# One more expert with 64 token slots, and another order of the experts, in a two-layer decoder trunk

## The chip, the cores and the metric

The kernel runs on one core of one Trainium2 chip. The metric is the device time of one execution in microseconds (us), the median of several runs. A measurement of this kernel can tell a change of about 0.2% (3 us) from none.

## What is computed

Two decoder layers over 256 tokens of width 1024, in float32. The change touches only the channel mixer of the second layer, a mixture of eight SwiGLU experts of which each token uses two:

```python
def _moe(h, w_router, w1, w3, w2):
    logits = (h @ w_router).astype(jnp.float32)
    top_v, top_i = lax.top_k(logits, TOP_K)          # TOP_K = 2 of N_EXPERTS = 8
    wts = jax.nn.softmax(top_v, axis=-1)
    ...
    for e in range(N_EXPERTS):
        y = y + gates[..., e:e + 1] * _swiglu(h, w1[e], w3[e], w2[e])
```

`_swiglu(h, w1, w3, w2)` is `(silu(h @ w1) * (h @ w3)) @ w2`, with a hidden width of 3584. One expert's three matrices are 3 x 1024 x 3584 floats, 42 MiB. 256 tokens times 2 make 512 choices. With the given inputs, the reference's routing gives expert 0 65 tokens and the other seven, sorted, 89, 75, 65, 63, 60, 48 and 47.

## The kernel before, in words

**Ahead of the experts** come dilated attention, the dense mixer and sliding-window attention; the change leaves them alone. The router then counts the tokens of each expert on the chip. Expert 0 always has rank 0. The other seven get ranks 1 to 7 by falling count (`route`, L1343).

**Slots.** An expert of rank r is computed for a fixed number of token slots, `CAPS[r]`, 96 or 64 (L31). `Expert` (L1140) builds a 0/1 matrix P on VectorE that says which token sits in which slot. For 64 slots it also copies P's 64 columns into the second half of the tile (L1152). `gather` (L1155) multiplies the normalised tokens by P on TensorE, which packs the expert's tokens into `xb`. `combine` (L1176) brings the results back to their tokens with P's transpose and adds them to the stream x. If a count is above its slots, `most` (L1441) is above 0, and a conditional block (L1466) computes all eight experts again for the tokens left over.

**Products of one expert.** The hidden width is cut into chunks of 1024, 1024, 1024 and 512 (`moe_chunks`). `hidden` (L1217) makes the products with w1 and w3 of one chunk into PSUM tiles H, `hidden_tail` (L1242) applies SiLU and the product and transposes the result on TensorE, and `output` (L1265) makes the products with w2 into PSUM tiles Y. Each TensorE instruction holds 32 token slots as the stationary operand and streams up to 512 weight columns, so the number of instructions goes with slots/32:

```python
for i in range(2):
    for g in range(ng):                    # ng = slots // 32
        mm32(H[i], g, x[g], a[i], **go)
    for g in range(4 - ng):
        mm32(H[i], ng + g, x[g], b[i], **go)
if ng == 3:                                # 96 slots: a third PSUM tile
    ...
```

That is 12 instructions for each 128 rows of a chunk of w1 and w3 with 96 slots and 8 with 64, and in `output` 6 and 4 for each 128 rows of w2. The trace shows each float32 product as two passes. The order on TensorE is H of chunk 0, H of chunk 1, Y of chunk 0, H of chunk 2, Y of chunk 1, H of chunk 3, Y of chunk 2, H of the next expert's chunk 0, Y of chunk 3.

**Weights.** All weights come through SyncE's DMA queue in tiles of 1 MiB, in the order in which TensorE uses them (`Stream`, L152). An expert takes 42 tiles, whatever its slots. The tiles rotate through 17 buffers: 5 called raw, 2 mwa, 10 mwb. SyncE issues a tile's DMA when the tile that held the buffer before has been used, and waits there in order. The eight experts run in two halves of four (`by_turn`, L1438 and L1511), in the order of `TURNS` (L32). Between the halves all engines read `most` and branch around the conditional block; by then the first 17 tiles of the second half have been asked for. In the last expert the ten mwb buffers are given up (`moe_cut`) after its third chunk's w1 and w3, and its last tiles and the four of the final gate matrix (`ple_w_gate`) pass through the other seven.

Of the kernel before, what the change touches and what calls it, by code (L numbers as in the profile page):

```python
# [27 lines left out]
FE = 3584  # L28
NE = 8

CAPS = (96, 96, 96, 96, 96, 96, 64, 64)  # L31
TURNS = (0, 6, 1, 2, 3, 4, 5, 7)  # L32
CAP = 96
BIG = 512.0
NRAW = 5
# [300 lines left out]
def trunk(ctx, tc, x, p, attn_norm, ffn_norm, a_w_qkv, a_w_o, kv_norm, kv_w, b_w_q, b_sinks,  # L336
# [70 lines left out]
    def add_moe(s, seq, at=None, extra=None):  # L407


        prev = None  # L410
        where = 0
        for j, item in enumerate(list(seq) + [None]):
            if item is not None:
                e, f0, fn = item
                nr = s.width * 128 // fn
                for r in range(0, D, nr):
                    for w in (moe_w1, moe_w3):
                        s.add(expert_rows(w, e, r, nr, f0, fn), "raw")
            if j == at:
                s.add(extra, "raw")  # L420
                where = len(s.specs)
            if prev is not None:
                e, f0, fn = prev
                for r in range(0, fn, s.width * 128 // D):
                    s.add(expert_rows(moe_w2, e, f0 + r, s.width * 128 // D, 0, D), "raw")
            prev = item
        return where
# [4 lines left out]
    def moe_seq(es):  # L432
        return [(e, f0, fn) for e in es for f0, fn in moe_chunks]
# [17 lines left out]
    moe0 = len(st.specs)  # L451
    ranks = [(r,) if r else 0 for r in TURNS]
    add_moe(st, moe_seq(ranks[:4]))
# [463 lines left out]
    if True:  # L917
# [127 lines left out]
        count, total, capx, capt = (rt.tile([128, NE], F32, name=n) for n in ("count", "total", "capx", "capt"))  # L1045
        for r, c in enumerate(CAPS):
            vec.memset(capt[:, r:r + 1], float(c))
# [3 lines left out]
        def warm(n):  # L1051

            t = scr()
            v = n_f1.h0[0]
            for _ in range(n):
                mm(t, v[:, :128], v, start=True, stop=True)
# [286 lines left out]
    def route():  # L1343
# [14 lines left out]
        if WARM2:  # L1358
            warm(WARM2)
        first.append(Expert(CAPS[0], posm[:, :, 0:1], by_rank[1][:, :, 0:1]))  # L1360
        vec.tensor_copy(count, ps[:, 16:24])
# [43 lines left out]
    def expert_pools(sb, ps, k):  # L1405

        nonlocal moep, psH, psY, psB
        moep = pool(f"moe{k}", 2, sb, side="right")
        psH = pool(f"psH{k}", 1, ps, space=PSUM)
        psY = pool(f"psY{k}", 1, ps, space=PSUM)  # L1410
        psB = pool(f"psS{k}", 2, ps, space=PSUM)
# [4 lines left out]
    def by_turn(turns, then={}, **kw):  # L1416

        def make(r):
            return lambda: Expert(CAPS[r], *(v[:, :, r:r + 1] for v in by_rank)) if r else first[0]

        experts([make(r) for r in turns], then=then, **kw)

    def find():

        flow.until(lambda: ranked)
        for r in TURNS:
            if r:
# [9 lines left out]
    expert_pools(moes, banks, 1)  # L1437
    by_turn(TURNS[:4], {(0, 0): find})  # L1438

# [70 lines left out]

    by_turn(TURNS[4:], {(3, PLE_AT - 1): load_p1, (3, PLE_AT): proj_p1}, nxt=n_p1.half)  # L1511
    st.phase(7)
# [89 lines left out]
```

## Time and profile before

| | |
|---|---|
| median of 3 runs | 1594.5 us (1593.62 to 1595.17) |
| the profiled execution | 1597.32 us |
| its span, first to last instruction | 1595.6 us |
| TensorE (PE) busy in it | 1542.3 us, 97% |
| DMA, mean of the span | 286 GB/s |
| expert weight tiles | 336 of 1024 KB |
| experts, first half | from about 631 us |
| experts, second half | from about 1095 us |
| tail after the last expert's hidden stages (final gate, norm, output) | from about 1530 us |

A row of a view by stretches gives, for each engine, its busy time in a stretch and in brackets its instructions; then the share of its clock that TensorE was granted, the busy share of the 16 DMA engines, and what they moved. A row of the chain gives a start, a duration and what ran: the chain is the work that ended last, followed back from the end, so it shows what the end waited for at each moment.

### The profile page before, as it was taken

What the parts mean: (1) busy time and instruction counts of PE and PEld (TensorE: products, weight loads), DVE (VectorE), ACT (ScalarE), POOL (GpSimd) and SP (SyncE); (2) the same over time, 40 slices, a digit from 0 to 9 for tenths busy, and PEclk for the clock granted to TensorE, in tenths of its full rate; (3) what the DMA queues carried; (4) which work ended last, traced back from release to release, by engine and by line L of the source; (5) the groups of instructions that cost most, each with busy time, mean ns of one, the idle gap of its engine ahead of it and who ended that gap; (6) DMA issues with size and microseconds to landing.
All of it is one profiled execution on the core that took longest, in us unless ns stands there. A gap on an engine that the chain in (4) does not pass through costs nothing. (4 is left out here: it accounts for less than half of the span.)

```text
span 1595.6 us, 29196 instructions
## 1 busy us (share of the span) xinstructions
PE 1542.3 (97%) x12326; PEld 874.3 (55%) x12326; DVE 549.3 (34%) x1286; ACT 437.4 (27%) x857; POOL 11.3 (1%) x22
## 2 busy tenths in 40 slices
PE   7999999999999999999999999987999999999977
PEld 6999889788888876333342333333343343343326
DVE  6776677654446793100201102111000200201124
ACT  5555555554445672100100101000000000001123
POOL 0000000000000000000000000000000000000000
PEclk9999999999999999999999999997999999999997
DMA  9544445565554434999999999996999999999880
GB/s 275 150 138 138 120 139 186 154 227 180 190 190 146 142 109 189 409 403 408 409 402 409 404 407 409 403 408 262 387 360 383 368 343 386 367 345 401 324 330 27
DMA packets 214586, 455.71 MB, mean 286 GB/s; under 512 B 15440, under 2 KB 97232, under 8 KB 214448
## 3 DMA queue, kind: packets, MB, share of 16 engines
q1 hardware_dynamic: 214128, 453.31, 77.0%
q8 instruction: 98, 1.61, 0.4%
q0 software_dynamic: 176, 0.40, 0.1%
q14 instruction: 40, 0.33, 0.1%
q10 hardware_dynamic: 144, 0.07, 0.0%
HBM read 452.69 MB, written 1.05 MB: 284 GB/s over the span
## 5 line engine op out<-in xcount | busy, mean ns | idle before, releaser
L1137 PE MATMUL H<-mwb,xb 128*32 128x512 f32 (+1 forms) x3320 | 337.7, 538 | 0.4 <-DMA mwb<-in_moe_w 0.4
L135 DVE TENSOR_TENSOR wlo<-raw,whi 128x768 fp32r<-128x768 f32 (+1 forms) x180 | 188.6, 1080 | 117.7 <-ACT whi L135 117.5
L135 DVE TENSOR_TENSOR sa<-sa,H 128x512 f32<-128x512 f32 (+1 forms) x32 | 19.9, 621 | 591.2 <-PE H L1137 591.2
L1137 PEld LDWEIGHTS H<-mwb,xb 128*32 128x32 f32 x3320 | 110.8, 110 | 203.0 <-issue 180.0
L135 ACT ACTIVATE whi<-raw 128x768 fp32r<-128x768 f32 (+1 forms) x180 | 162.0, 945 | 110.9 <-PE scr L347 61.3
L135 ACT ACTIVATE sa<-H 128x512 f32<-128x512 f32 (+1 forms) x32 | 17.4, 544 | 637.3 <-PE H L1137 637.3
L1137 PE MATMUL H<-raw,xb 128*32 128x512 f32 (+1 forms) x1560 | 168.5, 545 | 1.0 <-DMA raw<-in_moe_w 1.0
L1137 PE MATMUL Y<-mwb,hT 128*32 128x512 f32 x1304 | 150.8, 594 | 0.0
L1137 PE MATMUL Y<-raw,hT 128*32 128x512 f32 x904 | 105.6, 593 | 0.0
L1137 PEld LDWEIGHTS H<-raw,xb 128*32 128x32 f32 x1560 | 52.6, 110 | 95.5 <-issue 83.3
L347 PE MATMUL acc<-whi,xT0h 128*128 128x384 f32 (+2 forms) x296 | 104.1, 352 | 0.0
L347 PE MATMUL acc<-wlo,xT0h 128*128 128x384 f32 (+2 forms) x296 | 101.7, 344 | 1.6 <-DVE wlo L135 1.6
L347 PE MATMUL acc<-whi,xT0l 128*128 128x384 f32 (+2 forms) x296 | 101.5, 343 | 0.0
L347 PE MATMUL acc<-whi,xT1h 128*128 128x384 f32 (+2 forms) x280 | 98.2, 351 | 0.3 <-ACT xT1h L135 0.3
L347 PE MATMUL acc<-whi,xT1l 128*128 128x384 f32 (+2 forms) x280 | 93.8, 335 | 0.2 <-DVE xT1l L135 0.2
L347 PE MATMUL acc<-wlo,xT1h 128*128 128x384 f32 (+2 forms) x280 | 93.4, 334 | 0.0
L1137 PEld LDWEIGHTS Y<-mwb,hT 128*32 128x32 f32 x1304 | 41.7, 110 | 88.7 <-issue 86.7
L1137 PE MATMUL H<-mwa,xb 128*32 128x512 f32 (+1 forms) x752 | 88.9, 534 | 0.0
L1137 PEld LDWEIGHTS Y<-raw,hT 128*32 128x32 f32 x904 | 29.2, 110 | 62.4 <-issue 60.4
L347 PEld LDWEIGHTS acc<-whi,xT0h 128*128 128x128 f32 x296 | 56.5, 191 | 4.9 <-issue 2.3
L347 PEld LDWEIGHTS acc<-wlo,xT0h 128*128 128x128 f32 x296 | 56.3, 190 | 4.5 <-DVE wlo L135 2.3
L347 PEld LDWEIGHTS acc<-whi,xT0l 128*128 128x128 f32 x296 | 56.2, 190 | 3.0 <-DVE xT0l L135 0.3
(222 smaller groups left out, 1878.9 us busy)
## 6 DMA issues: line engine op xcount, KB each, us to landing
mwb<-in_moe_w SPq DMA_DIRECT2D x190, 1024.0 KB, 16.0
raw<-in_moe_w SPq DMA_DIRECT2D x104, 1024.0 KB, 13.9
mwa<-in_moe_w SPq DMA_DIRECT2D x42, 1024.0 KB, 15.1
raw<-in_a_w_qkv SPq DMA_DIRECT2D x144, 256.0 KB, 3.9
raw<-in_dense_w SPq DMA_DIRECT2D x33, 1024.0 KB, 5.0
raw<-in_ple_w_gate SPq DMA_DIRECT2D x8, 1024.0 KB, 9.6
raw<-in_a_w_o SPq DMA_DIRECT2D x4, 1024.0 KB, 5.1
raw<-in_b_w_q SPq DMA_DIRECT2D x4, 1024.0 KB, 5.2
```

What stands on the lines that cost most here:

```text
L135: f(*a, **k)
L347: nc.tensor.matmul(dst, lhsT, rhs, **kw)
L1137: nc.tensor.matmul(dst, xs, w, start=start, stop=stop)
```

## The change

The sixth entry of `CAPS`, the slots of rank 5, goes from 96 to 64, and `TURNS` is rearranged:

```diff
-CAPS = (96, 96, 96, 96, 96, 96, 64, 64)
-TURNS = (0, 6, 1, 2, 3, 4, 5, 7)
+CAPS = (96, 96, 96, 96, 96, 64, 64, 64)
+TURNS = (0, 5, 1, 2, 6, 3, 4, 7)
```

By slots, the order of the eight was 96, 64, 96, 96 and 96, 96, 96, 64. It is now 96, 64, 96, 96 and 64, 96, 96, 64. In the first half the instructions are the same ones (another expert's weights are read in the second place, and the table of slots holds another number). In the second half the first expert has 64 slots where it had 96. SyncE's list of DMAs is the same, row for row.

TensorE at the start of the second half, where the first expert's hidden stage begins (H_23211 to H_23213 are its PSUM tiles, mwb and raw the weight tiles, xb the gathered tokens):

```order
 L1137 MATMUL H_23211<-mwb,xb 32x512 x4
 L1137 MATMUL H_23212<-raw,xb 32x512 x4
-L1137 MATMUL H_23213<-mwb,xb 32x512 x2
-L1137 MATMUL H_23213<-raw,xb 32x512 x2
-L352 MATMUL scr<-ident,P 96x128 x2
+L352 MATMUL scr<-ident,P 128x128 x2
 L1137 MATMUL H_23211<-mwb,xb 32x512 x4
 L1137 MATMUL H_23212<-raw,xb 32x512 x4
-L1137 MATMUL H_23213<-mwb,xb 32x512 x2
-L1137 MATMUL H_23213<-raw,xb 32x512 x2
```

The third PSUM tile and its 4 of 12 instructions are gone for every 128 rows of this expert's weights.

VectorE at the same place, just after the branch: it builds P, on which TensorE's gather waits there. Before:

```order
L135 TENSOR_SCALAR P<-iota,posr 128x96 x2
L135 CAST PT<-scr 96x256
L135 TENSOR_TENSOR sa<-sa,H_23212 128x512
L135 TENSOR_TENSOR sb<-sb,H_23213 64x512
L135 COPY hT<-scr 128x256
```

Now:

```order
L135 TENSOR_SCALAR P<-iota,posr 128x64
L135 COPY P<-P 128x64
L135 TENSOR_SCALAR P<-iota,posr 128x64
L135 COPY P<-P 128x64
L135 CAST PT<-scr 128x256
L135 TENSOR_TENSOR sa<-sa,H_23212 128x512
```

Two copies stand between and after the two parts of P, and the work on the third PSUM tile (sb, and its hT) is gone.

## Rows read from the trace of the kernel before

**Rows 1.** The page: busy time of the engines; the chain that ended last, by line.
```profile
PE 1542.3 (97%) x12326; PEld 874.3 (55%) x12326; DVE 549.3 (34%) x1286; ACT 437.4 (27%) x857; POOL 11.3 (1%) x22
...
PE H L1137 17%; PE Y L1137 8%; PE scr L347 2%; PE acc L347 1%; DMA raw<-in_ple_w_gate 1%; PE scr L1258 1%; DVE wlo L135 0%; PE scr L352 0%; ACT xb L135 0%; DVE gate L135 0%; DVE h L135 0%; DVE x L135 0%; ACT gate L135 0%; DVE yl L135 0%; POOLq L1599 0%
```

**Rows 2.** Stretches: the first half, the halt at the branch, the second half.
```profile
core 0: us, PE busy (x) PEld busy (x) DVE busy (x) ACT busy (x) POOL busy (x), PEclk, DMA share, GB/s
640.00:1080.00 440.00, 432.04 (x4205) 152.31 (x4197) 53.91 (x101) 36.56 (x66) 0.00 (x0) 1.00 1.03 406
1093.00:1100.00 7.00, 7.00 (x61) 3.43 (x64) 0.42 (x1) 0.65 (x2) 0.00 (x0) 0.94 0.01 3
...
1120.00:1480.00 360.00, 359.22 (x3516) 127.84 (x3512) 44.50 (x79) 29.03 (x54) 0.00 (x0) 1.00 0.97 372
```

**Rows 3.** What SyncE's DMA queue waited for, 1100 to 1500 us: total, times, longest.
```profile
SPq L230 <- PE H L1137: 198.9, 63, 7.5
SPq L230 <- PE Y L1137: 107.2, 43, 7.1
```

**Rows 4.** Stretches of PE: 64 slots, 96 after it, two of the second half's 96.
```profile
743.50:828.60 85.10, 84.96 (x820) 1.00 1.03 406
828.60:948.90 120.30, 118.58 (x1161) 1.00 1.03 407
1207.30:1328.20 120.90, 120.57 (x1178) 1.00 0.97 365
1328.20:1448.90 120.70, 120.58 (x1180) 1.00 0.96 366
```

**Rows 5.** What PE itself waited for by DMA, 828 to 949 us.
```profile
PE H L1137 <- DMA raw<-in_moe_w: 1.0, 1, 1.0
PE H L1137 <- DMA mwb<-in_moe_w: 0.4, 1, 0.4
```

**Rows 6.** The chain in the second half: start us, us, what.
```profile
1231.47 0.98 PE scr L1258 x8
...
1270.36 20.60 PE H L1137 x192
1290.96 1.97 PE scr L347 x16
...
1411.90 1.93 PE scr L347 x16
...
1417.21 10.44 PE Y L1137 x96
1427.65 10.36 PE H L1137 x192
...
1466.22 0.59 PE scr L1258 x4
...
1494.78 13.73 PE H L1137 x128
...
1516.02 7.00 PE Y L1137 x64
1523.02 6.52 PE H L1137 x120
```

**Rows 7.** Timeline of VectorE and TensorE at the branch; P's readers there (min/median/max ns).
```profile
1088.52 0.45 DVE L135 TENSOR_SCALAR P<-iota,posr 128x96 f32<-128x96 f32 x2 [5.77 <-DVEq L1466]
...
1088.94 6.14 PE L347 MATMUL scr<-P,xn 128*128 128x96 f32 x32 [6.97 <-DVE P L135]
...
L347 PEld LDWEIGHTS scr<-P,xn x32: 192/333/333, 1088.9 to 1094.7; 128*128 128x128 f32 x32
```

**Rows 8.** Timeline of SyncE's DMA issues: at the branch, and in the last expert.
```profile
1054.36 46.90 SPq L230 DMA_DIRECT2D mwb<-in_moe_w  x10
1101.51 10.65 SPq L230 DMA_DIRECT2D raw<-in_moe_w  x5
...
1488.40 7.23 SPq L230 DMA_DIRECT2D mwa<-in_moe_w  x2
1515.61 7.84 SPq L230 DMA_DIRECT2D raw<-in_moe_w  x5
```

**Rows 9.** Line L230's DMAs from 600 us on: time from issue to landing.
```profile
DMA to landing us min/median/max: 5.0/15.2/21.8
```

## The prediction

> **What bounds the kernel now.** The page says TensorE is busy 97% of the span and heads the chain that ended last, with the experts' H and Y products as its largest parts [rows 1]. That is an average, so the next view is by stretches [rows 2]. It shows two different states. In the first half of the experts the DMA engines run without a break, at 406 GB/s. In the second half they move 372 GB/s and have pauses, although TensorE is as busy as before. What SyncE waits for tells which of the two limits the second half: for 199 us on H products and 107 us on Y products [rows 3]. It waits until TensorE has used a tile and its buffer comes free. So in the second half TensorE sets the pace, and the transfers follow. There TensorE waited for a transfer for only 1.4 us in all, in the expert after the 64-slot one [rows 5], so both are close to their limits. The second half is where the change takes work away.
>
> **What the change removes.** One expert of 96 slots becomes one of 64. The stretches give its worth in one step. From one expert's first hidden product to the next one's takes 120.9 and 120.7 us for 96 slots in the second half, and 85.1 us for the 64 slots of the first half, whose neighbours were both 96 as well [rows 4]: 35.7 us less. The last Y products of an expert fall into the next one's stretch, so that stretch is shorter too: 120.3 us, of which TensorE was busy 118.58 [rows 4]. In it TensorE waited for transfers for 1.4 us [rows 5]. Without that it is 118.9, or 1.9 less than 120.8. Sum: 37.6 us.
>
> The same from below, as a check [rows 6]. H of a full chunk is 192 passes in 20.60 us with 96 slots and 128 in 13.73 with 64, so 6.87 less, three times: 20.6. The half chunk is 192 passes of 256 columns in 10.36 us; two thirds of it is 6.9, so 3.5 less (of those 128 passes the chain shows 120 in 6.52 us). Y is 96 passes in 10.44 us against 64 in 7.00, so 3.44 for a full chunk, and 3.5 chunks: 12.0. The transposes of a hidden chunk take 0.98 us against 0.59; 0.39 times 3.5 is 1.4. Together 37.5 us. All of it lies on TensorE, and in the second half TensorE's time is the chain without a gap, so the end moves by the same amount as long as the weights keep up (below).
>
> **What it adds and moves.** VectorE builds P at the branch with two copies more. One stands between the two parts of P. TensorE's gather starts right after the first part and would need the second part at its second product [rows 7]. The trace has no such copy; the bounds are 0 and 0.27 us, the length of one part of P (0.45 us for two that overlap). I take 0.2 us, since a copy of 64 columns is nearest to a part of P with 96.
>
> The gather at the branch has 64 columns in place of 96. It took 6.14 us for 32 passes, 0.192 us each, and the shortest weight load there took the same 192 ns, so the loads, which don't change, set its pace [rows 7]. Bounds: 0, and a third of 6.14 us, 2.0 us less. A pair of warm gathers decides: 16 passes took 1.97 us with 96 columns and 1.93 us with 64 [rows 6]. I take 0.1. The Trainium skill (TensorE: Matmul & The Clock Gate, "Wait — 56ns, not 53.3ns?") says that back-to-back matmuls start a number of columns divided by the clock apart; by that the gather would shrink by a third, and the sum be 2 us better. The warm pair shows 2% and not a third, so it is not followed here.
>
> The work of ScalarE and VectorE on the third PSUM tile goes too. I cost that at nothing: TensorE is busy 359.2 of 360 us beside it [rows 2]. In the first half a 64-slot expert stands between two of 96, and TensorE has 0.14 us of idle time in its 85.1 [rows 4]; a new wait at these seams is bounded by that, and the other seams keep their neighbours.
>
> **Whether the weights keep up.** This is the term that can eat the gain. The transfers do not shrink: 42 tiles for each expert. At 406 GB/s [rows 2] a tile of 1.0486 MB takes 2.58 us, 108.5 us for an expert. A 96-slot expert takes longer than that (120.8), a 64-slot one less (85.1). So a 64-slot expert eats into the tiles that wait in the buffers, 23 us of them, and a 96-slot one gives back 12.
>
> At the branch all 17 buffers have been filled: DMA falls to 3 GB/s at 1093 to 1100 us [rows 2]. Transfers start again when TensorE releases the first pair of tiles, at 1100.9 (the last of ten issues that end at 1101.3) [rows 8]. A transfer alone takes 5.0 us [rows 9], so tile 18 lands at 1105.9 and each one after it 2.58 us later if SyncE never waits for long. TensorE reaches the second expert of the half, which needs tile 42, at 1207.3 before [rows 4] and at about 1171.6 after. Tile 42 lands at 1105.9 + 24 x 2.58 = 1167.8. That is 3.8 us early. In the two 96-slot experts that follow the lead grows again by about 12 us each. The other close place is in the last expert, up to tile 161, the last one before SyncE halts for the seven buffers that are left (it waited there from about 1495 to 1515.6 before [rows 8]). Tile 161 lands at 1105.9 + 143 x 2.58 = 1474.8, and is needed when the last hidden chunk begins: 1523.0 before [rows 6], 1485.5 after. That is 10.7 us early. From there on each transfer is started by a release, as before, and the tail keeps its shape. So the end should move by the full amount, but the pace may not fall below 143 tiles in 379.6 us, 2.655 us each or 395 GB/s.
>
> **The sum.** -37.6 + 0.2 - 0.1 = -37.5 us. Of the profiled execution's 1597.3 us that leaves 1559.8. The same difference from the median of the runs, 1594.5, gives **1557.0 us**.
>
> **The rivals.**
>
> *The transfers become the bound.* Below 395 GB/s the end is late by 143 x (1048.6 / pace - 2.655) us with the pace in GB/s. For it: the second half moved only 372 GB/s. At that pace the tile takes 2.819 us, the end is 23.4 us late, and the time is 1580. Against it: SyncE was waiting for buffers in those 372 [rows 3], and without such long waits it held 406 GB/s over 440 us [rows 2]. The Trainium skill (HBM Reference, "Specifications") speaks against the change: it gives a core about 358 GB/s of its memory's bandwidth. By that the tile would take an estimated 2.93 us, the end would be 39 us late and the gain gone, at 1596. It is a share for two cores at work at once, and the trace's 406 GB/s with one at work stands against it. A mild form, 400 to 393 GB/s, costs 0 to 2 us. I give the whole case 0.07, most of it for the mild form to 1562.
>
> *The overflow block runs.* This is the one that ends slower. It decides at L1466: if the expert of rank 5 has 65 tokens or more, all eight experts are computed again. 336 tiles at 2.58 us are 867 us more at least, about 2424 us. The counts speak against it: 60 tokens of rank 5 with these inputs, four below the point. The chance is 0.01.
>
> *The narrow expert is no shorter, or the seams between widths wait.* For it would speak idle time around the 64-slot expert of the first half; there is 0.14 us [rows 4]. If each of the two new neighbours waited as long as the gather waits at the branch for P (0.4 us) or some us for a combine, 1558 to 1562. If the expert were not shorter at all, the time would stay at 1594.5. The first has 0.04, the second 0.01.
>
> **How the numbers follow.** The forecast gets 0.87. Its own bounds are 2 us less (the gather, all of its third), 1 us either way for the two sums and the runs' own spread (1593.6 to 1595.2), and upward 0.2 us of copies and the 1.4 us of short waits that the first half had. That makes 1554.5 to 1559.5. The range reaches on to the mild forms of the first and third rival, 1562. About 0.2% of this kernel, 3 us, is what a measurement can tell from no change. Faster by more than that: the forecast, the third rival's seams and all of the first rival but its far end, 0.97. Within: the far end of the first rival and the expert that is not shorter, 0.015. Slower: the overflow and what I have not thought of, 0.015.
>
> **What would show it.** In the changed kernel's profile the first half should look the same. In the second half the stretch of the first expert should be about 76 us where it was 112 (1095.0 to 1207.3), the next one about 119, the other two as before. The DMA rate from 1105 us on should be at 400 GB/s or more, against 372, with far less waiting of SyncE on H and Y products. TensorE's waits for transfers should stay at some 2 us in all. The SyncE halt in the last expert should be there still, shorter than 20 us, since the transfers arrive with less lead. The tail after the last hidden chunk should have the same length. Wrong would be: waits of TensorE for mwb, raw or mwa tiles of 5 us or more, at the second expert's start or in the last expert, with a DMA rate under 395 GB/s; a second pass over the weights after the branch; or idle TensorE at the seams between widths, ended by VectorE or ScalarE.

## The result, and the profile after

The changed kernel takes **1558.87 us** (median of four runs, 1557.69 to 1559.65). Beside it the kernel before took 1594.84 us (four runs, 1593.62 to 1595.63). The ratio is 0.9773, with a 95% interval of 0.9761 to 0.9785, so the change saves 36.0 us. The forecast was 1557.0 us with a range of 1554.5 to 1562.

The profiled execution of the changed kernel took 1557.69 us, and its span is 1555.9 us. Its stretches of TensorE, cut at the experts' first hidden products, at the last hidden chunk and at the end (columns as in [rows 2]):

```profile
1093.90:1171.90 78.00, 77.86 (x755) 27.73 (x758) 3.69 (x8) 5.72 (x11) 0.00 (x0) 0.98 0.95 372
1171.90:1290.30 118.40, 118.06 (x1160) 42.16 (x1156) 11.69 (x21) 8.67 (x16) 0.00 (x0) 1.00 1.03 407
1290.30:1411.00 120.70, 120.59 (x1182) 42.94 (x1178) 16.09 (x29) 9.72 (x18) 0.00 (x0) 1.00 1.03 406
1411.00:1484.90 73.90, 73.90 (x608) 23.48 (x604) 10.41 (x15) 8.91 (x15) 0.00 (x0) 1.00 0.95 370
1484.90:1555.90 71.00, 50.14 (x374) 31.30 (x366) 27.88 (x48) 24.02 (x49) 2.83 (x4) 0.87 0.45 171
```

Three of the same stretches before, the ones that are not among [rows 4]:

```profile
1095.00:1207.30 112.30, 111.96 (x1121) 40.42 (x1124) 7.74 (x16) 7.98 (x15) 0.00 (x0) 1.00 0.92 349
1448.90:1522.80 73.90, 73.90 (x608) 23.50 (x604) 10.38 (x15) 8.91 (x15) 0.00 (x0) 1.00 0.91 354
1522.80:1595.60 72.80, 51.63 (x374) 32.14 (x366) 28.06 (x48) 24.01 (x49) 2.83 (x4) 0.84 0.43 166
```

Read down, they say where the time came from:

| Stretch | before, us | after, us | difference | forecast |
|---|---|---|---|---|
| up to the second half's first hidden product | 1095.0 | 1093.9 | -1.1 | +0.1 |
| second half, first expert (now 64 slots) | 112.3 | 78.0 | -34.3 | -35.7 |
| second expert (96) | 120.9 | 118.4 | -2.5 | -1.9 |
| third expert (96) | 120.7 | 120.7 | 0 | 0 |
| fourth expert (64), up to its last hidden chunk | 73.9 | 73.9 | 0 | 0 |
| from there to the end | 72.8 | 71.0 | -1.8 | 0 |

The two stretches that were to move by more than 1 us, the narrow expert's and the one behind it, hold -36.8 us, and the other four together hold -2.9. The two profiled executions differ by 39.6 us, the medians by 36.0. The profiled execution of before stood 2.5 us above its median and that of after 1.2 below its own, so the -2.9 is of the size by which single executions scatter, and no step of the change is read from it.

The second question was whether the weights keep up. One stretch of the second half, after:

```profile
1105.00:1450.00 345.00, 344.41 (x3336) 121.28 (x3326) 40.76 (x71) 27.96 (x51) 0.00 (x0) 1.00 1.03 407
```

The last number is 407 GB/s where [rows 2] had 372 in 1120 to 1480 us: the transfers now run without pauses, as they did in the first half. What SyncE waited for there (1100 to 1465 us, the two largest rows):

```profile
SPq L230 <- PE H L1137: 94.5, 56, 5.3
SPq L230 <- PE Y L1137: 59.4, 29, 4.6
```

That is 154 us in place of the 306 of [rows 3]. The six smaller rows of the same list add 35 us. TensorE's own waits in the second half, 1100 to 1490 us, have no transfer among them; the whole list is one row:

```profile
PE scr L352 <- ACT xb L135: 0.2, 1, 0.2
```

### The profile page after: what moved, and what is told of

It reads as the page before. It is cut to its first block, busy times and chain, and to the rows that moved or that the text cites. A ratio compares the mean times of both kernels' runs of the same rounds, so it can differ in the third digit from the quotient of the medians.

```text
span 1555.9 us, 28406 instructions
## 1 busy us (share of the span) xinstructions
PE 1507.0 (97%) x11944; PEld 862.5 (55%) x11944; DVE 541.2 (35%) x1274; ACT 433.9 (28%) x851; POOL 11.3 (1%) x22
## 5 line engine op out<-in xcount | busy, mean ns | idle before, releaser
L1137 PE MATMUL H<-mwb,xb 128*32 128x512 f32 (+1 forms) x3176 | 322.9, 540 | 0.2 <-DMA mwb<-in_moe_w 0.2
L135 DVE TENSOR_TENSOR wlo<-raw,whi 128x768 fp32r<-128x768 f32 (+1 forms) x180 | 188.5, 1079 | 117.8 <-ACT whi L135 117.5
L1137 PEld LDWEIGHTS H<-mwb,xb 128*32 128x32 f32 x3176 | 104.9, 110 | 194.3 <-issue 169.7
L1137 PE MATMUL H<-raw,xb 128*32 128x512 f32 (+1 forms) x1480 | 158.8, 546 | 0.0
L1137 PE MATMUL Y<-mwb,hT 128*32 128x512 f32 x1240 | 143.4, 594 | 0.0
L1137 PEld LDWEIGHTS H<-raw,xb 128*32 128x32 f32 x1480 | 49.4, 110 | 90.7 <-issue 79.7
L1137 PE MATMUL Y<-raw,hT 128*32 128x512 f32 x856 | 99.7, 593 | 0.0
L1137 PE MATMUL H<-mwa,xb 128*32 128x512 f32 (+1 forms) x720 | 82.7, 531 | 0.0
```

The lines of the kernel that those rows point to most:

```text
L135: f(*a, **k)
L1137: nc.tensor.matmul(dst, xs, w, start=start, stop=stop)
```

## Experiments

Every edit is shown against the changed kernel. All eight ran beside the kernel before, at 1595.5 us in one group and 1595.9 in the other.

### The order alone, and the slots alone

Order alone:

```diff
-CAPS = (96, 96, 96, 96, 96, 64, 64, 64)
+CAPS = (96, 96, 96, 96, 96, 96, 64, 64)
```

> The new order with the slots of before: 96, 96, 96, 96 and 64, 96, 96, 64. Theory A: TensorE's work is that of the kernel before, and the transfers keep up in both halves, so the time is that of before, 1593 to 1598 us; the second half takes what it takes in the changed kernel, the first half about 36 us more. Rival (the order alone brings part of the gain): under 1590 us.

Measured: 1594.10 us (1592.0 to 1597.35), ratio 0.9991 (0.9981 to 1.0). The order is worth nothing by itself, as long as there are two narrow experts.

Slots alone, with the order of before, by which both narrow experts of the second half stand at its end (96, 96, 64, 64):

```diff
-TURNS = (0, 5, 1, 2, 6, 3, 4, 7)
+TURNS = (0, 6, 1, 2, 3, 4, 5, 7)
```

> The third 64-slot expert stays, the order of before comes back, so that by slots the order is 96, 64, 96, 96 and 96, 96, 64, 64. Theory A (TensorE sets the pace only as long as tiles wait in the buffers; a 64-slot expert uses up about 23 us of that lead, a 96-slot one gives 12 us back): the two 64-slot experts at the end use up the lead of about 41 us that the second half reaches, TensorE waits 14 to 20 us for tiles in the last expert, and the time is 1573 to 1579 us, some 17 above the changed kernel. Rival B (only the number of slots counts, the order is idle): 1557 to 1561 us, and no such waits.

Measured: 1573.48 us (1571.88 to 1574.74), ratio 0.9861 (0.9845 to 0.9878). The same removed work gives 22 us in place of 36. TensorE's waits for transfers in the second half, 1040 to 1500 us, which the changed kernel does not have:

```profile
PE H L1137 <- DMA mwb<-in_moe_w: 7.8, 6, 1.5
PE H L1137 <- DMA raw<-in_moe_w: 2.3, 2, 1.5
PE Y L1137 <- DMA mwb<-in_moe_w: 0.6, 1, 0.6
PE H L1137 <- DMA mwa<-in_moe_w: 0.6, 1, 0.6
```

They add up to 11.3 us of the 14.6 between the two orders; the other 3.3 us these rows do not place. All of them come after 1410 us, in the last expert, where theory A had put them, but they are below its 14 to 20 us. So the order is worth 14.6 us, and only once the slots are cut: it sets where the lead of the weights is spent. Two narrow experts in a row spend twice 23 us of it and win nothing back between them.

### A smaller lead

Six mwb buffers in place of ten, so that 13 tiles can be in flight or waiting and not 17:

```diff
-NMB = 10
+NMB = 6
```

> The changed kernel with 6 mwb buffers in place of 10, so 13 tiles of lead and not 17. Theory A: the lead is 10.3 us shorter. In the changed kernel the tightest tile at the second half's second expert came 6 to 7 us early, and at the first half's third expert 2 to 3 us, so TensorE now waits about 4 to 5 us at each of the two: 1565 to 1570 us. Rival (tiles in flight at the DMA's full rate are all that counts, and 13 buffers hold enough of them): 1557 to 1561 us.

Measured: 1564.31 us (1562.59 to 1567.26), ratio 0.9803 (0.9787 to 0.982). That is 5.4 us over the changed kernel, just below the lower end of what the lead theory gave and outside its rival's. The stretch of the second half's first expert grows from 78.0 to 81.9 us, and TensorE's waits for transfers after 1040 us are:

```profile
PE H L1137 <- DMA raw<-in_moe_w: 2.2, 2, 1.5
PE H L1137 <- DMA mwb<-in_moe_w: 0.7, 2, 0.5
PE Y L1137 <- DMA raw<-in_moe_w: 0.6, 1, 0.6
PE Y L1137 <- DMA mwb<-in_moe_w: 0.5, 1, 0.5
```

They are 4.0 us, and 3.2 us more stand in the first half. The lead decides, but each buffer is worth less than the 2.58 us of a tile: four buffers are 10.3 us of transfer and cost 5.4. With all 17, the pair of tiles that the second expert starts on had landed 5.0 us before its use (rows under "The weights keep up"), less than the 6 to 7 us that the expectation took. 10.3 less 5.0 is 5.3. That this slack took up the difference is likely, and was not tried by itself.

### A fourth narrow expert

The expert of rank 4 (63 tokens) gets 64 slots too, and wide and narrow ones alternate throughout:

```diff
-CAPS = (96, 96, 96, 96, 96, 64, 64, 64)
-TURNS = (0, 5, 1, 2, 6, 3, 4, 7)
+CAPS = (96, 96, 96, 96, 64, 64, 64, 64)
+TURNS = (0, 4, 1, 5, 6, 2, 3, 7)
```

> A fourth expert, rank 4 with its 63 tokens, gets 64 slots; by slots the order is 96, 64, 96, 64 and 64, 96, 96, 64. A count by TensorE's work alone would take another 37 us off: 1521 us. Theory A: the lead of the buffers runs out in the first half's last expert and again at the start of the second half's second expert, TensorE waits about 21 us for tiles, and 1540 to 1545 us come out, 17 below the changed kernel. Rival C (the changed kernel is at the limit of the transfers already, so that less work on TensorE buys nothing): 1556 to 1560 us.

Measured: **1547.22 us** (1546.28 to 1548.01), ratio 0.9694 (0.9678 to 0.971). It is the fastest version of all, 11.7 us below the changed kernel, and still 2.2 us above the expected range: of the 36 to 37 us that a narrow expert is worth, a third is left. The first half of the experts:

```profile
640.00:1050.00 410.00, 394.42 (x3803) 137.56 (x3795) 43.23 (x78) 30.85 (x58) 0.00 (x0) 1.00 1.03 406
```

The transfers run without a pause, and TensorE is idle for 15.6 us, 14.0 of them waiting for a transfer. The transfers have become the bound there. The other loss is one wait that the expectation had not priced. TensorE's timeline at the branch (start us, us, what; in brackets the idle time ahead of it and what ended it):

```profile
1092.52 3.64 PE L1137 MATMUL H<-mwb,xb 128*32 128x512 f32 x16 [8.94 <-ACT sa L135]
```

ScalarE's step that TensorE waits for, and SyncE's last issue ahead of the branch and first one behind it:

```profile
1091.87 0.60 ACT L135 ACTIVATE sa<-H 128x512 f32<-128x512 f32 x1 [24.03 <-SPq L1466]
```

```profile
1073.92 1.80 SPq L230 DMA_DIRECT2D mwb<-in_moe_w  x1
...
1092.03 0.39 SPq L230 DMA_DIRECT2D mwb<-in_moe_w  x1
```

ScalarE's first SiLU step behind the branch waits for SyncE's side of the branch (L1466). SyncE had its tiles to ask for until 1075.7 us, and 16.3 us passed from there to the first issue behind the branch. What SyncE waited for at the branch (total, times, longest), and how long the tile of its last issue took to land:

```profile
SPq L1466 <- SPq L1466: 15.8, 6, 5.2
```

```profile
DMA to landing us min/median/max: 17.7/17.7/17.7
```

That tile landed at 1091.6 us, and SyncE went on right after it. The ones ahead of it show the same: tiles landed at 1081.6, 1084.2, 1086.7 and 1089.2 us, and steps of SyncE at L1466 follow at 1081.7, 1084.2, 1086.7 and 1089.2. So SyncE stands at the branch until every tile that it has asked for has landed. With a narrow expert on both sides of the branch TensorE is there before it: it has no PSUM tile for the next product until ScalarE has read one.

### SyncE let through earlier

To separate that wait, the same four narrow experts, with only 11 of the 17 tiles asked for ahead of the branch and the rest behind it:

```diff
+        self.limit = 1 << 30
...
-        while self.loaded < len(self.specs):
+        while self.loaded < min(self.limit, len(self.specs)):
...
+    st.limit = moe0 + 4 * 42 + 11
...
+    main.limit = 1 << 30
```

> The kernel with four 64-slot experts, but at most 11 of the second half's tiles are asked for ahead of the branch, in place of 17. Theory A (in the kernel with four, SyncE reached the branch only when the last of the 17 tiles had been issued, at the DMA's pace, and ScalarE and so TensorE then waited 9 us for SyncE's side of the branch): SyncE passes about 15 us earlier, that wait goes, and 1547 becomes 1537 to 1541 us. Rival (the wait was the transfers' own, the tiles were simply late): TensorE waits as long for tiles, and the time stays at 1546 to 1549 us or rises.

Measured: 1548.9 us (1547.96 to 1550.03), ratio 0.9709 (0.9694 to 0.9723): no gain. The wait itself went, as meant. ScalarE's step now runs 8.6 us earlier, behind TensorE's product and no longer behind SyncE:

```profile
1083.26 0.60 ACT L135 ACTIVATE sa<-H 128x512 f32<-128x512 f32 x1 [14.92 <-PE H L1138]
```

But SyncE was at the branch for 19.3 us in its turn. Its last issue ahead of the branch and its first behind, and how long the tile of that last issue took to land:

```profile
1056.59 2.15 SPq L231 DMA_DIRECT2D mwb<-in_moe_w  x1
1078.09 1.00 SPq L231 DMA_DIRECT2D mwb<-in_moe_w  x2
```

```profile
DMA to landing us min/median/max: 20.7/20.7/20.7
```

The tile landed at 1077.3 us, and again SyncE went on only then. So theory A had only half of the reason: SyncE comes late to the branch, but what holds it there is the wait for the tiles under way, and that wait comes whenever it gets there. With nothing asked for meanwhile, the transfers ran dry; a stretch of 10 us:

```profile
1070.00:1080.00 10.00, 10.00 (x86) 2.73 (x82) 0.42 (x1) 0.00 (x0) 0.00 (x0) 0.92 0.40 137
```

TensorE paid that back afterwards (waits for transfers from 1040 to 1500 us):

```profile
PE H L1138 <- DMA raw<-in_moe_w: 3.9, 3, 1.7
PE H L1138 <- DMA mwb<-in_moe_w: 3.7, 4, 1.5
PE H L1138 <- DMA mwa<-in_moe_w: 3.6, 3, 1.5
PE Y L1138 <- DMA mwb<-in_moe_w: 2.4, 4, 0.7
PE Y L1138 <- DMA raw<-in_moe_w: 1.6, 3, 0.6
```

15.2 us of such waits stand where the fourth narrow expert with all 17 tiles had 4.1 and the one of 8.94. SyncE's time at the branch is paid either way, as a late ScalarE or as a gap in the transfers.

### The gather at the branch

The narrow expert's stretch was 1.4 us longer than forecast, and the rows at the branch show why. TensorE's timeline after, from the gather on:

```profile
1086.88 7.06 PE L347 MATMUL scr<-P,xn 128*128 128x64 f32 x32 [6.89 <-DVE P L135]
1093.87 1.94 PE L1137 MATMUL H<-mwb,xb 128*32 128x512 f32 x8
1095.58 1.69 PE L1137 MATMUL H<-raw,xb 128*32 128x512 f32 x8
```

And before, the first two groups behind the gather of [rows 7]:

```profile
1095.00 1.07 PE L1137 MATMUL H<-mwb,xb 128*32 128x512 f32 x8
1095.88 1.04 PE L1137 MATMUL H<-raw,xb 128*32 128x512 f32 x8
```

The granted clock (the number ahead of the last two) in 1092 to 1096 us, before and then after:

```profile
1092.00:1096.00 4.00, 4.00 (x31) 3.31 (x34) 0.00 (x0) 0.98 (x2) 0.00 (x0) 0.76 0.08 26
```

```profile
1092.00:1096.00 4.00, 4.00 (x22) 2.34 (x25) 0.00 (x0) 0.38 (x1) 0.00 (x0) 0.50 0.02 4
```

When the gather begins, the clock is at 0.50, the level of 1.2 GHz, in both kernels. (In the changed one it was there already in 1074 to 1079 us, among the last short products of the first half.) In the kernel before it rises 4.9 us into the gather. In the changed one it is still at 0.50 when the first hidden products run, and these take 1.94 and 1.69 us, not 1.07 and 1.04. At this level a pass of the gather takes the same time in both: 4 us hold 19 passes with 96 columns and 20 with 64 (the gather's instructions alone, before and then after):

```profile
1089.00:1093.00 4.00, 4.00 (x19) 4.00 (x20) 0.00 (x0) 0.50 0.55 201
```

```profile
1087.00:1091.00 4.00, 4.00 (x20) 4.00 (x20) 0.00 (x0) 0.50 0.54 203
```

So the gather's extra 0.9 us are the longer time at the lower clock; at one level of the clock the columns make no difference to a pass. One experiment gives every gather 96 columns of P again and uses only the 64 that are wanted:

```diff
+            gm = 96
...
-                        mm(t[:, m * c:m * (c + 1)], n_f1.xn[tb][:, 128 * (4 * q + c):128 * (4 * q + c + 1)],
-                           self.P[:, tb, :m], start=tb == 0, stop=tb == 1)
+                        mm(t[:, gm * c:gm * (c + 1)], n_f1.xn[tb][:, 128 * (4 * q + c):128 * (4 * q + c + 1)],
+                           self.P[:, tb, :gm], start=tb == 0, stop=tb == 1)
```

> The changed kernel, but every gather multiplies by 96 columns of P as with 96 slots, and only 64 of them are copied on for a 64-slot expert. In the four profiles with a 64-column gather at the branch the granted clock rose 10.0 to 11.5 us after that gather began, in the two with 96 columns 3.9 to 5.0 us after. Theory A (the narrower gather brought the late rise): the clock rises within 6 us, the first products of the expert there run at full clock, and the time is 1 to 3 us less, 1556 to 1558 us. Rival (when the clock rises there is chance, or the branch's doing): it rises after 10 us or more, and the time is 1558.5 to 1560 us.

Measured: 1558.48 us (1555.41 to 1559.34), ratio 0.9762 (0.9748 to 0.9775). That lies between the two ranges, at the edge of the rival's. In the trace theory A's effect is there:

```profile
1088.67 5.50 PE L347 MATMUL scr<-P,xn 128*128 128x96 f32 x32 [7.17 <-DVE P L135]
1094.10 1.06 PE L1137 MATMUL H<-mwb,xb 128*32 128x512 f32 x8
```

```profile
1092.00:1096.00 4.00, 4.00 (x35) 2.47 (x34) 0.00 (x0) 0.77 (x2) 0.00 (x0) 0.97 0.05 17
1094.10:1170.70 76.60, 76.46 (x757) 27.58 (x759) 3.69 (x8) 5.72 (x11) 0.00 (x0) 1.00 0.97 379
```

The gather is shorter with more columns (5.50 us against 7.06), the clock is up at the first hidden product, and the first expert's stretch is 76.6 us, the 76 that had been forecast. In the median it is 0.4 us (1.8 by the ratios to the kernel before), less than the runs scatter, so what the clock costs in time is not shown by it; by the rows it is 1.4 us of the stretch and 1.6 of the gather.

The other experiment keeps 64 columns and puts three products that nothing reads ahead of the branch:

```diff
+    t = scr()
+    for _ in range(3):
+        mm(t, ident, xt[0][:, half(0)], start=True, stop=True)
```

> The changed kernel with three products that nothing reads, put on TensorE ahead of the branch, where it idles from 1082 to 1087 us. Theory A (TensorE's clock at the branch costs 2 to 3 us): the clock is up when the gather begins or soon after, the gather takes 4 to 5 us in place of 7.1, and the time is 2 to 4 us less, 1555 to 1557 us. Rival: the products delay the gather by as much as they give, 1558 to 1561 us.

Measured: 1559.96 us (1556.9 to 1561.18), ratio 0.9777 (0.9764 to 0.979): no gain, so theory A missed, and the time is in the rival's range. Two stretches of it:

```profile
1083.00:1089.00 6.00, 2.46 (x13) 1.39 (x12) 0.81 (x4) 0.00 (x0) 0.94 (x2) 1.00 0.64 247
1092.00:1096.00 4.00, 4.00 (x20) 2.03 (x23) 0.00 (x0) 0.38 (x1) 0.00 (x0) 0.50 0.02 4
```

The clock came up before the gather and fell again during it, so the first hidden products ran at 0.50 as in the changed kernel. The gather was shorter, 5.72 us against 7.06, but began 1.0 us later.

### The overflow block

The expert of rank 3, with 65 tokens, gets 64 slots, so that one token is left over and the conditional block runs:

```diff
-CAPS = (96, 96, 96, 96, 96, 64, 64, 64)
+CAPS = (96, 96, 96, 64, 96, 64, 64, 64)
```

> The changed kernel with 64 slots for rank 3 too, which has 65 tokens, so that one token is left over and the conditional block runs. The prediction's lower bound for its price was 867 us, 336 tiles at the DMA's pace. The block loads through two buffers of half the size and starts no product ahead, so I expect well above that: 2450 to 3200 us in all. If the block were skipped or handled only the one expert, the time would stay under 1700 us.

Measured: 4333.91 us in one run, far above the expected range. The stretch of the block:

```profile
1100.00:3800.00 2700.00, 1585.79 (x9068) 416.59 (x9070) 115.49 (x198) 74.26 (x135) 0.00 (x0) 0.75 0.38 128
```

TensorE waits for tiles for 1046 us of these 2700. The block moves 128 GB/s, not 406: it has a stream of weights of its own, with two buffers. At that pace 336 tiles of 1.0486 MB take 2752 us, which is the 2775 us that were added, to 1%.

## Why the prediction was right, step by step

**TensorE sets the pace of the second half, so removed work comes out in full.** Right. The medians moved by 36.0 us for a forecast 37.5. In the two profiled executions the two stretches concerned became 36.8 us shorter, for a forecast 37.6. The third expert and the fourth up to its last hidden chunk kept their lengths to 0.1 us. (The 1.4 us of waits for transfers that the prediction names beside the second half are the first half's; [rows 5] are of 828 to 949 us.)

**What a narrow expert saves.** The whole of 37.6 us was taken from the first half's 64-slot expert and the one behind it [rows 4]. The second stretch gave 2.5 us where 1.9 were forecast, and the first 34.3 where 35.7 were. The narrow expert of the first half, which is the model for it, took 85.0 us again (743.1 to 828.1 us).

**The mis-sized term is the work at the branch.** The copies of P were put at 0.2 us and the gather at -0.1. The copies cost nothing: TensorE waited 6.89 us for P against 6.97 [rows 7], with VectorE's first part of P, a copy and the second part in 0.6 us:

```profile
1086.48 0.25 DVE L135 TENSOR_SCALAR P<-iota,posr 128x64 f32<-128x64 f32 x1 [5.69 <-DVEq L1466]
1086.77 0.20 DVE L135 COPY P<-P 128x64 f32<-128x64 f32 x1
1086.87 0.25 DVE L135 TENSOR_SCALAR P<-iota,posr 128x64 f32<-128x64 f32 x1
```

The gather grew by 0.9 us, from 6.14 to 7.06, and the first two groups of hidden products by 1.5, since they ran at the lower clock. The step that failed is the bound "0, and a third of 6.14 us, 2.0 us less": it counted what fewer columns might save, from a warm pair, and left out that the clock might rise later. Its reading of [rows 7] hid this: 0.192 us a pass is the mean over two levels of the clock, about 0.21 us at 0.50 and 0.12 at full clock [rows 6], and that it equals the shortest weight load is chance, for the median load there took 333 ns. The forecast's own bounds, up to 1559.5 (1554.1 to 1559.6 if its terms are added up), held the time by the 1 us and the short waits that they had for other things; for this term that is luck. The rule on columns and clock in the Trainium skill (TensorE: Matmul & The Clock Gate, "Wait — 56ns, not 53.3ns?"), by which the gather would have shrunk by a third, does not set its pace here: 20 and 19 passes with 64 and 96 columns fill 4 us at 0.50, and 16 take 1.93 and 1.97 us at full clock [rows 6].

**The weights keep up.** Right, by a margin near the one worked out. The pace was 407 GB/s where 395 were needed, and TensorE had no wait for a transfer in the second half up to the last hidden chunk. The prediction's tile 42, of the pair that the second expert starts on, in SyncE's list and then its time to landing:

```profile
1148.31 2.23 SPq L230 DMA_DIRECT2D mwa<-in_moe_w  x1
```

```profile
DMA to landing us min/median/max: 18.6/18.6/18.6
```

It landed at 1166.9 us, 5.0 us before TensorE's first product of that expert at 1171.9 (forecast 3.8 us). SyncE's transfers had begun at 1098.7 us where 1100.9 was taken. SyncE's halt in the last expert is still there, and shorter: from 1463.1 to 1477.7 us, 14.7 us against 20.0. The last tile ahead of it is the 160th, not the 161st, and it landed at 1476.8 us, 8.1 us before the last hidden chunk began (forecast 10.7 us).

**The rivals.** The transfers did not become the bound: they held 407 GB/s over 345 us. The Trainium skill (HBM Reference, "Specifications") says that a core streaming alone gets well above its share of about 358 GB/s, and this trace, with 407, agrees. But the rival was nearer than its 0.07 says. With the order of before it happens (1573.48 us), with 13 buffers it begins (1564.31), and with one narrow expert more it takes two thirds of the gain. The overflow did not run; its price was given as 867 us at least, from 406 GB/s, and it is 2775. The seams between widths show no idle time: TensorE is busy 77.86 of 78.00 us and 118.06 of 118.40.

## What to carry to other kernels

Where computing and loading are nearly equal, ask of a cut in one of them how long the other can live on its lead, place by place: the same cut gave 22 us with its light parts next to each other and 36 with them apart. The next cut of that kind gave 12, so the balance point is worth working out beforehand: 42 tiles of 2.58 us are 108.5 us for an expert, and TensorE's mean for an expert is (5 x 120.8 + 3 x 85.1) / 8 = 107.4 us with three narrow ones, so only the lead at the start was left to spend. A synchronisation point such as a branch that all engines take is a place where the engines that wait are not the ones that were looked at: there, read every engine's first instruction behind it. Here the queue that issues the transfers also waits at the branch for every tile under way, whichever way the issues are split around it.

## What was not expected of the hardware

- **With fewer columns in the gather the clock at the branch rose later.** This is one profiled execution of each kernel. In all five kernels with 64 columns there and no products put ahead (the changed one, the order alone, six buffers, and the two with a fourth narrow expert) the first hidden products ran at the lower clock, at about 1.9 us for eight instructions. In the three with 96 columns (before, slots alone, wide gather) they took 1.06 or 1.07 us. Their gathers took 5.50 to 6.14 us, the others' 7.06. The length of the idle time ahead of the gather does not explain it: a fourth gather with 96 columns, in the kernel whose overflow block runs, took 5.65 us behind 1.39 us of idle time. Three more products ahead of the branch did not help. Why the clock rises later is not settled.
- **SyncE passes the branch only when the tiles that it has asked for have landed.** That takes 16 to 19 us, from its last issue ahead of the branch to the first behind, where TensorE stands some 7 us, and ScalarE's first SiLU step waits for it. With three narrow experts SyncE is through at 1091.1 us, before TensorE's first hidden product at 1093.9, and TensorE does not wait for it.
